# Norm of x: where the transposes' products lie, and when exp of a_log runs

## The chip, the cores and the metric

One core of one Trainium2 chip runs the whole program. The metric is the device time of one execution in microseconds (us); lower is better. Engines: PE is TensorE, whose matmuls show as PE and whose weight loads show as PEld; DVE is VectorE, ACT is ScalarE, POOL is GpSimd, and SP issues most transfers.

## The reference, cut to what matters

The program is one step of a hybrid decoder layer. What is computed around the change:

```python
def _rmsnorm(x, g):
    xf = x.astype(jnp.float32)
    xf = xf * lax.rsqrt(jnp.mean(xf * xf, axis=-1, keepdims=True) + EPS)
    return (xf * g.astype(jnp.float32)).astype(x.dtype)

def _layer(x, ...):
    hn = _rmsnorm(x, norm_g)
    proj = hn @ w_in                     # 1024 -> 13344 columns
    u, v, gate_a, z, xbc, dt_raw, q, gate_x, merge = jnp.split(proj, ...)
    ...
    dt = jax.nn.softplus(dt_raw + dt_bias)
    a = -jnp.exp(a_log)
    y, h_new = _ssd(xh, dt, a, ...)      # decays from cumulative sums of dt * a
    ...
```

The rows of x are 512 of a prompt and 64 of samples; the sizes are D_MODEL 1024, 32 SSD heads, SSD chunks of 128.

## The kernel before, in words

The kernel keeps everything transposed: the model dimension on the 128 partitions, the 576 rows of x along the free axis. Every large product is made from fp32 split into a high and a low part in fp32r (`split`, L96: ACT copies the high part, DVE subtracts), so a block of 128 output columns costs, for each of two halves of 288 rows (`HT`), 24 matmuls: three for each of the 8 pieces of the model dimension (`gemm`, L141, its matmul at L154; `gemm_half`, L159, at L167).

**Order of the work.** A planner lays out each engine's instructions ahead of time, from the program's order and its own guess of durations; the chip then runs each engine's list in that order, with waits between engines. The order on an engine therefore is not the order of the source, and an edit can move instructions that it does not name. A tile of a pool is a buffer that the planner hands out when its first writer is placed, and takes back when its last reader is placed.

**Banks.** In the first part of the kernel, PE's results have 8 banks (`banks(stb, 4, 1, 3)`, L189): 4 for accumulators (`acc_tile`, L71), 1 for `y_tile`, and 3 for small products (`s_tile`, L77). A tile of any kind is one bank of 128 x 512 fp32.

**Norm of x** (L195 to L240). Five tiles of x (four of 128 rows, one of 64) are loaded. Two groups follow one another, tiles 0 to 2 and tiles 3 to 4. For each group: ACT squares and sums (L226); `rsqrt_` (L101) makes the factor, with a Sqrt on ACT (L109); DVE scales the tiles (L230). Then, for each of the 8 pieces k of the model dimension, PE transposes that piece of every tile of the group into one bank (L237), ACT writes the high part `hn_hi` from it, times the norm's weight (L239), and DVE writes the low part `hn_lo` from the same bank (L240). The bank is free again when both have read it. In the first group a piece is 384 columns wide, in the second 192.

**What follows.** The product for dt (L287, 48 matmuls of 32 output columns at L154) needs all of hn: its first half of 288 rows needs the first group alone. ACT adds the bias (L290), PE transposes (L293), and DVE and ACT make softplus of it (L296 to L313): an Exp on ACT at L301, a series on DVE. Then exp of a_log on ACT (L315), dt times that on DVE (L317), and cumulative sums on PE (L319 to L322). The first blocks of xBC are multiplied by `gemm_half` (L167) in between. Sqrt and Exp need different function tables on ACT; a table load is put ahead of the first instruction in ACT's order that needs another table. In the kernel before, that is a_log's Exp (L315).

The helper `run(first, *made)` (L118) orders an instruction behind others; within one engine it only fixes the order there.

Of the kernel before, what the change touches and what calls it, by code (L numbers as in the profile page):

```python
# [11 lines left out]
AF = mybir.ActivationFunctionType  # L12
# [30 lines left out]
def tile_hybrid_step(  # L43
# [8 lines left out]
    V, S, PE, GP, SY = nc.vector, nc.scalar, nc.tensor, nc.gpsimd, nc.sync  # L52
# [18 lines left out]
    def acc_tile():  # L71
        return bank["acc"].tile([P, 512], F32, tag="acc", name="acc")
# [4 lines left out]
    def s_tile():  # L77
        return bank["sps"].tile([P, 512], F32, tag="sps", name="sps")
# [22 lines left out]
    def rsqrt_(pool, r, a, b, tag="nwt", root=False):  # L101

        sh = [r.shape[0], r.shape[1]]
        w = pool.tile([P, P], F32, tag=tag, name="nwt", bufs=2)[:, 0:24].rearrange("p (k c) -> p k c", k=3)
        x, y, t = (w[:sh[0], k, 0:sh[1]] for k in range(3))
        V.tensor_scalar(x, r, a, b, ALU.mult, ALU.add)
        if root:
            V.reciprocal(y, x)
            S.activation(y, y, AF.Sqrt)  # L109
        else:  # L110
            V.tensor_scalar(y.bitcast(I32), x.bitcast(I32), -0.5, 1597463007.0, ALU.mult, ALU.add)
        for _ in range(1 if root else 3):
            V.tensor_tensor(t, y, y, ALU.mult)
            V.scalar_tensor_tensor(t, t, -0.5, x, ALU.mult, ALU.mult)
            V.scalar_tensor_tensor(y, t, 1.5, y, ALU.add, ALU.mult)
        return y

    def run(first, *made):  # L118

        for m in made:  # L120
            tc.add_manual_dep(first.ins, m.ins.name, mybir.DependencyInfo(
                mybir.DependencyClass.NoSync if m.ins.engine == first.ins.engine else mybir.DependencyClass.Sync,
                mybir.DependencyReason.DATA), reason="run")
# [17 lines left out]
    def gemm(w, nk, xh, xl, n=P, width=HT, halves=2):  # L141

        hi, lo = w
        outs = []
        for f in range(halves):
            ps = acc_tile()
            sl = slice(f * width, (f + 1) * width)
            last = 3 * nk - 1
            i = 0
            terms = [[(hi[:, k], xh(k)), (hi[:, k], xl(k)), (lo[:, k], xh(k))] for k in range(nk)]  # L150
            if lo_last[0]:
                terms = [t[0:2] for t in terms] + [t[2:3] for t in terms]
            for a, b in [p for t in terms for p in t]:
                PE.matmul(ps[:n, :width], lhsT=a, rhs=b[:, sl], start=(i == 0), stop=(i == last))  # L154
                i += 1
            outs.append(ps)
        return outs
# [30 lines left out]
    with ExitStack() as stb:  # L188
# [30 lines left out]
        for tiles in ((0, 1, 2), (3, 4)):  # L219
            n = len(tiles)  # L220
            ss = pb.tile([P, 3], F32, tag="ss", name="ss", bufs=2)
            if 4 in tiles:
                GP.memset(ss, 1.0)
            for a, i in enumerate(tiles):
                m = TS if i == 4 else P
                S.activation(junk[:m], xts[i][:m], AF.Square, accum_out=ss[:m, a:a + 1])  # L226
            q = rsqrt_(pb, ss[:, 0:n], 1.0 / D, EPS, "BT", root=True)
            for a, i in enumerate(tiles):
                m = TS if i == 4 else P
                V.tensor_scalar_mul(xts[i][:m], xts[i][:m], q[:m, a:a + 1])  # L230
            c0 = tiles[0] * P
            w = 3 * P if n == 3 else P + TS
            for k in range(KD):
                ps = s_tile()
                for a, i in enumerate(tiles):
                    m = TS if i == 4 else P
                    PE.transpose(ps[:, a * P:a * P + m], xts[i][:m, k * P:(k + 1) * P], ident[:m, :m])  # L237
                g = gcol[:, k:k + 1]
                S.activation(hn_hi[:, k, c0:c0 + w], ps[:, 0:w], AF.Copy, scale=g)  # L239
                V.scalar_tensor_tensor(hn_lo[:, k, c0:c0 + w], ps[:, 0:w], g, hn_hi[:, k, c0:c0 + w], ALU.mult, ALU.subtract)  # L240
# [26 lines left out]
        alog = pb.tile([P, H], F32, name="alog")  # L267
# [19 lines left out]
        ps = gemm(wdt, KD, xh, xl, n=H)  # L287
# [10 lines left out]
        tmp = pb.tile([P, 3, HC], F32, tag="cacc", name="tmp", bufs=2)  # L298
        sa, sb, sc = tmp[:, 0], tmp[:, 1], tmp[:, 2]
        V.scalar_tensor_tensor(sa, dtr, -1.0, dtr, ALU.mult, ALU.max)  # L300
        S.activation(sa, sa, AF.Exp, scale=-1.0)  # L301
        V.tensor_scalar(sb, sa, 2.0, None, ALU.add)
        V.reciprocal(sb, sb)
        V.tensor_tensor(sa, sa, sb, ALU.mult)
# [7 lines left out]
        dtf = dt.rearrange("p c h -> p (c h)")  # L312
        V.scalar_tensor_tensor(dtf, sc, 2.0, dtr, ALU.mult, ALU.add)  # L313
        V.memset(dt[64:128, 4, :], 0.0)
        S.activation(alog, alog, AF.Exp)  # L315
        adt = pb.tile([P, 5, H], F32, tag="t1", name="adt", bufs=2)
        V.scalar_tensor_tensor(adt, dt, -1.0, alog[:, None, :].to_broadcast([P, 5, H]), ALU.mult, ALU.mult)  # L317
        aps = s_tile()
# [1130 lines left out]
    for i in range(4):  # L1449
# [6 lines left out]
        for p_, (c0, cn) in enumerate(pieces):  # L1456
            ps = acc_tile()
# [54 lines left out]
```

## Time and profile before

| what | us |
|---|---|
| median of 3 runs | 1135.39 |
| lowest and highest of them | 1131.92, 1139.5 |
| the profiled execution, its own time | 1134.07 |
| its span, from the first to the last instruction | 1132.3 |
| TensorE busy in the span | 1099.1 |
| mean granted TensorE clock | 0.993 |

The profiled execution's time is 1.8 us more than its span: what lies around the instructions. An engine's timeline gives for each instruction its start, its duration, and in brackets how long the engine had been idle before it and what ended that. Matmuls are pipelined: a matmul's duration is longer than the distance to the next one, so it is the distance between starts that says how fast PE goes. Busy times of PE are modelled from such ends.

### The profile page before, as it was taken

What the parts mean: (1) busy time and instruction counts of PE and PEld (TensorE: products, weight loads), DVE (VectorE), ACT (ScalarE), POOL (GpSimd) and SP (SyncE); (2) the same over time, 40 slices, a digit from 0 to 9 for tenths busy, and PEclk for the clock granted to TensorE, in tenths of its full rate; (3) what the DMA queues carried; (4) which work ended last, traced back from release to release, by engine and by line L of the source; (5) the groups of instructions that cost most, each with busy time, mean ns of one, the idle gap of its engine ahead of it and who ended that gap; (6) DMA issues with size and microseconds to landing.
All of it is one profiled execution on the core that took longest, in us unless ns stands there. A gap on an engine that the chain in (4) does not pass through costs nothing.

```text
span 1132.3 us, 20429 instructions
## 1 busy us (share of the span) xinstructions
PE 1099.1 (97%) x8200; PEld 1022.9 (90%) x8200; DVE 781.2 (69%) x1444; ACT 618.5 (55%) x1291; POOL 25.3 (2%) x109
## 2 busy tenths in 40 slices
PE   5999898999999999999999999999999999999997
PEld 4999797999999999999999778999999999889776
DVE  5679686858678786876536546877965567775743
ACT  6366686777767576775543236335652335564421
POOL 1010000000000000000000000000000000000000
PEclk9999999999999999999999999999999999999999
DMA  5343535254452525445224515441262453456311
GB/s 174 113 101 114 143 113 142 64 174 111 145 149 82 161 62 175 111 144 149 80 88 141 174 67 185 149 149 38 90 218 96 154 161 112 138 171 205 141 47 74
DMA packets 160334, 144.38 MB, mean 128 GB/s; under 512 B 10152, under 2 KB 141264, under 8 KB 160240
## 3 DMA queue, kind: packets, MB, share of 16 engines
q1 hardware_dynamic: 137136, 125.60, 36.6%
q10 hardware_dynamic: 23104, 17.49, 4.9%
q8 instruction: 64, 1.05, 0.4%
q14 instruction: 30, 0.25, 0.1%
HBM read 123.61 MB, written 19.46 MB: 126 GB/s over the span
## 4 chain that ended last, share of the span: by engine, by line
PE 88%; DMA 4%; DVE 3%; ACT 2%; issue 1%; SPq 0%; ACTq 0%; DVEq 0%
PE acc L167 35%; PE acc L926 16%; PE acc L154 12%; PE acc L1056 4%; PE acc L1461 4%; DMA e<-a_scr 3%; PE acc L1121 2%; PE yps L556 2%; PE sps L575 1%; PE sps L652 1%; PE sps L511 1%; PE sps L600 1%; PE sps L540 1%; DVE cacc L426 1%; PE yps L1409 1%
## 5 line engine op out<-in xcount | busy, mean ns | idle before, releaser
L167 PE MATMUL acc<-hn_hi,whi 128*128 128x288 f32 x896 | 272.3, 304 | 0.1
L167 PE MATMUL acc<-hn_hi,wlo 128*128 128x288 f32 x896 | 266.5, 297 | 1.5 <-DVE wlo L99 1.5
L167 PE MATMUL acc<-hn_lo,whi 128*128 128x288 f32 x896 | 266.4, 297 | 0.0
L167 PEld LDWEIGHTS acc<-hn_hi,whi 128*128 128x128 f32 x896 | 170.4, 190 | 1.9 <-issue 1.5
L167 PEld LDWEIGHTS acc<-hn_hi,wlo 128*128 128x128 f32 x896 | 170.1, 190 | 2.0 <-DVE wlo L99 2.0
L167 PEld LDWEIGHTS acc<-hn_lo,whi 128*128 128x128 f32 x896 | 170.5, 190 | 0.4
L98 ACT CAST w<-wraw 128x1024 fp32r<-128x1024 f32 (+1 forms) x64 | 59.2, 942 | 103.2 <-PE acc L926 24.0
L99 DVE TENSOR_TENSOR wlo<-wraw,whi 128x1024 fp32r<-128x1024 f32 x72 | 87.8, 1220 | 29.1 <-ACT whi L98 28.7
L167 PE MATMUL acc<-hb,whi 128*128 128x288 f32 x512 | 104.5, 299 | 0.1
L98 ACT CAST whi<-wraw 128x1024 fp32r<-128x1024 f32 x72 | 75.6, 1050 | 46.1 <-PE acc L167 44.0
L99 DVE TENSOR_TENSOR w<-wraw,w 128x1024 fp32r<-128x1024 f32 x64 | 68.5, 1087 | 35.8 <-ACT w L98 35.3
L926 PE MATMUL acc<-hn_hi,w 128*128 128x288 f32 x512 | 89.4, 301 | 0.0
L926 PE MATMUL acc<-tT,w 128*128 128x288 f32 x576 | 86.2, 298 | 0.0
L426 DVE SCALAR_TENSOR_TENSOR cacc<-raw,cwh,cacc 128x600 f32<-128x600 f32 x96 | 80.4, 838 | 4.7 <-ACT cacc L424 4.0
L167 PEld LDWEIGHTS acc<-hb,whi 128*128 128x128 f32 x512 | 81.6, 188 | 1.0 <-issue 0.6
L926 PEld LDWEIGHTS acc<-tT,w 128*128 128x128 f32 x576 | 78.6, 188 | 0.9 <-issue 0.9
L926 PEld LDWEIGHTS acc<-hn_hi,w 128*128 128x128 f32 x512 | 74.1, 188 | 2.0 <-DVE thx L944 0.4
L167 PE MATMUL acc<-hb,wlo 128*128 128x288 f32 x256 | 75.3, 294 | 0.0
L499 ACT ACTIVATE e<-e,nacs 128x128 f32<-128x128 f32 (+1 forms) x160 | 50.4, 382 | 13.4 <-DVE e L497 13.0
L99 DVE TENSOR_TENSOR w<-S,w 128x1024 fp32r<-128x1024 f32 x32 | 39.1, 1223 | 25.0 <-ACT w L98 25.0
L154 PE MATMUL acc<-ha,w 128*128 128x288 f32 x384 | 51.6, 295 | 0.0
L154 PE MATMUL acc<-hn_hi,w 128*128 128x288 f32 x256 | 51.2, 295 | 0.0
(393 smaller groups left out, 2117.5 us busy)
## 6 DMA issues: line engine op xcount, KB each, us to landing
wraw<-in_w_in_dram SPq DMA_DIRECT2D x44, 1024.0 KB
wraw<-in_w_in_dram SPq DMA_DIRECT2D x16, 512.0 KB
e<-a_scr SPq DMA_DIRECT2D x32, 256.0 KB
h<-in_state_ssm_dram SPq DMA_DIRECT2D x16, 512.0 KB
out_dram<-h ACTq DMA_DIRECT2D x16, 512.0 KB
wraw<-in_w_proj_b_dram SPq DMA_DIRECT2D x8, 1024.0 KB
ebc<-e_scr SPq DMA_DIRECT2D x16, 288.0 KB
wraw<-in_w_mem_kv_dram SPq DMA_DIRECT2D x4, 1024.0 KB
```

Of the source, the lines that this page charges most:

```text
L98: S.copy(hi, v)
L99: (e or V).tensor_tensor(lo, v, hi, ALU.subtract)
L154: PE.matmul(ps[:n, :width], lhsT=a, rhs=b[:, sl], start=(i == 0), stop=(i == last))
L167: PE.matmul(ps[:, 0:HT], lhsT=a[:, k], rhs=b(k)[:, sl], start=(n == 0), stop=(n == 3 * nk - 1))
L426: V.scalar_tensor_tensor(a[:, 0:n], raw[:, i:i + n], cwh[:, i, q:q + 1], a[:, 0:n], ALU.mult, ALU.add)
L499: S.activation(e[:, h, 0:w], e[:, h, 0:w], AF.Exp, bias=nacs[:, c, h0_ + h:h0_ + h + 1])
L511: PE.transpose(tp[:, j * P:(j + 1) * P], xs[:, j, c0:c0 + P], ident)
L556: m = PE.matmul(y4[64 * r:64 * r + 64, i, j], lhsT=xdt[:, h], rhs=e[:, h, 0:w], start=True, stop=True)
L926: PE.matmul(ps[:, 0:HT], lhsT=w[:, r, k], rhs=x(q, k), start=first and n == 0, stop=n == 11, skip_group_check=True)
L1056: PE.matmul(pss[i], lhsT=x(k)[:, c], rhs=w[:, r, k2], start=(k + q == 0), stop=(k == KD - 1 and q == 2))
L1121: PE.matmul(pss[i], lhsT=x[xr], rhs=w[:, r, k2], start=(k + q == 0), stop=(k == KD - 1 and q == 2))
L1461: PE.matmul(ps[:, 0:cn], lhsT=x(k)[:, c], rhs=w, start=(k + q == 0), stop=(k == KD - 1 and q == 2))
```

## The change

Two edits. In the norm of x, the bank for piece k is taken from the three banks for small products when k is odd, and from the four accumulators' banks when k is even, so that up to 7 banks serve the transposes in place of 3. And exp of a_log (L315) is ordered on ACT behind the Exp of softplus (L301).

```diff
             for k in range(KD):
-                ps = s_tile()
+                ps = s_tile() if k % 2 else acc_tile()
                 for a, i in enumerate(tiles):
                     m = TS if i == 4 else P
                     PE.transpose(ps[:, a * P:a * P + m], xts[i][:m, k * P:(k + 1) * P], ident[:m, :m])
...
         V.scalar_tensor_tensor(sa, dtr, -1.0, dtr, ALU.mult, ALU.max)
-        S.activation(sa, sa, AF.Exp, scale=-1.0)
+        made = S.activation(sa, sa, AF.Exp, scale=-1.0)
         V.tensor_scalar(sb, sa, 2.0, None, ALU.add)
...
         V.memset(dt[64:128, 4, :], 0.0)
-        S.activation(alog, alog, AF.Exp)
+        run(S.activation(alog, alog, AF.Exp), made)
         adt = pb.tile([P, 5, H], F32, tag="t1", name="adt", bufs=2)
```

## Rows read from the trace of the kernel before

**Rows 1.** The page: busy time of each engine, and the last chain by engine.
```profile
PE 1099.1 (97%) x8200; PEld 1022.9 (90%) x8200; DVE 781.2 (69%) x1444; ACT 618.5 (55%) x1291; POOL 25.3 (2%) x109
PE 88%; DMA 4%; DVE 3%; ACT 2%; issue 1%; SPq 0%; ACTq 0%; DVEq 0%
```
**Rows 2.** Stretches: start:end, length, each engine's busy us (instructions), TensorE clock, DMA.
```profile
13.20:18.35 5.15, 4.95 (x22) 4.10 (x22) 4.50 (x9) 3.75 (x8) 0.38 (x2) 1.00 0.77 198
18.35:27.20 8.85, 7.95 (x51) 5.12 (x49) 5.82 (x14) 5.83 (x13) 0.00 (x0) 1.00 0.08 19
46.00:49.00 3.00, 3.00 (x15) 3.00 (x14) 1.95 (x6) 2.20 (x5) 0.00 (x0) 0.50 0.49 138
99.00:219.00 120.00, 111.28 (x885) 104.66 (x884) 95.45 (x193) 85.32 (x211) 3.98 (x22) 0.97 0.43 121
```
**Rows 3.** Timeline of PE: start, us, engine, line, output<-inputs, [idle before <-releaser].
```profile
10.69 2.23 PE L237 MATMUL sps<-ident,xbuf 128*128 128x128 f32 x9 [8.07 <-DVE xbuf L230]
13.16 0.45 PE L154 MATMUL acc<-hn_hi,whi 128*32 128x288 f32 x1 [0.24 <-ACT hn_hi L239]
13.81 0.90 PE L237 MATMUL sps<-ident,xbuf 128*128 128x128 f32 x3 [0.20 <-DVE hn_lo L240]
...
14.99 0.84 PE L237 MATMUL sps<-ident,xbuf 128*128 128x128 f32 x3
...
15.87 0.44 PE L154 MATMUL acc<-hn_lo,whi 128*32 128x288 f32 x1
16.11 0.84 PE L237 MATMUL sps<-ident,xbuf 128*128 128x128 f32 x3
...
18.52 0.29 PE L154 MATMUL acc<-hn_lo,whi 128*32 128x288 f32 x1
18.65 0.29 PE L154 MATMUL acc<-hn_hi,wlo 128*32 128x288 f32 x1
...
18.91 0.49 PE L237 MATMUL sps<-ident,xbuf 128*128 128x128 f32 x3
...
20.75 0.32 PE L154 MATMUL acc<-hn_hi,whi 128*32 128x288 f32 x1 [0.30 <-ACT hn_hi L239]
...
22.88 0.32 PE L154 MATMUL acc<-hn_hi,whi 128*32 128x288 f32 x1 [0.42 <-ACT hn_hi L239]
...
40.00 0.46 PE L319 MATMUL sps<-adt,tri 128*128 128x128 f32 x2
...
47.05 0.44 PE L167 MATMUL acc<-hn_hi,wlo 128*128 128x288 f32 x1
47.29 0.44 PE L167 MATMUL acc<-hn_hi,whi 128*128 128x288 f32 x1
```
**Rows 4.** Timeline of ACT: the two table loads, and the instructions beside the second.
```profile
0.80 1.28 ACT L213 ACT_TABLE_LOAD   x1 [0.80 <-PEq L1498]
...
18.71 1.28 ACT L315 ACT_TABLE_LOAD   x1
20.00 0.23 ACT L315 ACTIVATE alog<-alog 128x32 f32<-128x32 f32 x1
20.14 0.56 ACT L239 ACTIVATE hn_hi<-sps,gcol 128x384 fp32r<-128x384 f32 x1
...
30.07 0.49 ACT L290 ACTIVATE dtF<-acc,dtb 32x288 f32<-32x288 f32 x1
32.14 0.34 ACT L301 ACTIVATE tmp<-tmp 128x160 f32<-128x160 f32 x1 [1.58 <-DVE tmp L300]
```
**Rows 5.** Timeline of DVE: the end of the first group, and the last step of dt.
```profile
20.73 0.62 DVE L240 SCALAR_TENSOR_TENSOR hn_lo<-sps,gcol,hn_hi 128x384 fp32r<-128x384 f32 x1 [0.54 <-ACT hn_hi L239]
21.27 0.74 DVE L230 TENSOR_SCALAR xt<-xt,nwt 64x1024 f32<-64x1024 f32 x1
...
39.52 0.33 DVE L317 SCALAR_TENSOR_TENSOR adt<-dt,alog 128x160 f32<-128x160 f32 x1
```
**Rows 6.** Timeline of POOL: the write that the first ACTIVATE at L213 reads.
```profile
0.94 0.20 POOL L84 MEMSET ones<- 128x128 f32 x1
```

## Prediction, made before the run

> **What bounds the kernel now.** First the page: PE is busy for 97% of the span and holds 88% of the chain that ended last, ACT for 55% and DVE for 69% [rows 1]. So an instruction taken from ACT or DVE is worth only what PE waits for it, and a bank only what PE waits for banks. What can be won is idle time of PE, or time in which its clock is low, between its first transposes at 10.69 us and the end of the norm near 27 us.
>
> Second the timeline of PE in that stretch [rows 3]. Nine transposes go out (three pieces k of three tiles: that is all that 3 banks hold), then PE idles 0.24 us, does one matmul of dt, idles 0.20 until DVE has read the first bank, and from 13.81 goes in rounds: three transposes, two matmuls of dt. From 14.99 to 16.11 a round takes 1.12 us. In it PE does not idle: the stretch 13.20 to 18.35 has 4.95 us busy of 5.15 [rows 2]. The matmuls of dt fill what the banks leave open. Later there are two more gaps, 0.30 and 0.42 us, both ended by ACT's `hn_hi` [rows 3]; the whole stretch 18.35 to 27.20 has 8.85 - 7.95 = 0.90 us idle [rows 2]. Idle in all: 0.24 + 0.20 + 0.90 = 1.34 us.
>
> Third the clock. Matmuls of 288 columns start 0.24 us apart at 15.87 and 0.13 us apart at 18.52 [rows 3]. The granted clock is printed as 1.00 for both, but 0.24 is also their distance from 47.05 to 47.29 [rows 3], where 0.50 is granted [rows 2]. I go by the distance: PE is at its lower level, 1.2 GHz, until some 18.35 us, and at 2.4 GHz after it. In the 7.7 us from 10.69 to 18.35 the low level costs about half, 3.6 us: more than all the idle time.
>
> Fourth ACT and DVE. Between two `hn_hi` of the first group ACT loads a table, 1.28 us, and runs a_log's Exp, 0.23 us [rows 4]. The last transposes of that group start at 18.91 and last 0.49, so their bank was full at 19.40, and ACT came to it at 20.14 [rows 3, 4]. DVE's `hn_lo` at 20.73 waits for it, and the scaling of the last tile of x stands behind that, at 21.27 [rows 5].
>
> **The Exp moved.** Out of the norm go 1.28 + 0.23 = 1.51 us of ACT. Last in this place is then the transposes' end at 19.40, so `hn_hi` of the last piece starts 20.14 - 19.40 = 0.74 us earlier, and with it `hn_lo` and the last scaling. PE had dt's matmuls to do until about 20.45, so it gains the gap of 0.30 and a part of the other 0.60 idle. Lower bound 0, upper bound 0.90; I take 0.6.
>
> The load comes back ahead of softplus's Exp at L301. ACT is done at 30.07 + 0.49 = 30.56 and idles 1.58 us until 32.14 [rows 4]. A load needs no data of its instruction: the one at L213 starts at 0.80, before POOL writes at 0.94 what that instruction reads [rows 4, 6]. So 1.28 us fit into 1.58, with 0.30 to spare, and a_log's Exp (0.23) follows L301 and is wanted only at 39.52 [rows 5]. Price 0. If the cover is gone, the load starts when L301 could: 1.28 us late for the whole series on DVE. That series ends at 39.52 + 0.33 = 39.85, and PE takes it up at 40.00 without having idled [rows 3, 5]: only 0.15 us of slack in PE's list, so the loss would be up to 1.28 - 0.15 = 1.1 us.
>
> The Trainium skill speaks against this part: ScalarE: Activation LUTs, What ACT_TABLE_LOAD costs, counts about 1283 ns for the load and about 1380 more for a drain, 2.66 us for each change of table. By that the load would not fit into 1.58 us, but come 1.08 us late and cost some 0.9 us at L319. This trace agrees on the load alone: 1.28 us, and its Exp starts 0.01 us after its end; no drain is seen in it [rows 4].
>
> **The banks.** With 7 banks PE need not stop after nine transposes. A transpose at the low level costs (1.12 - 2 x 0.24) / 3 = 0.213 us. The 15 left of the first group end at 12.92 + 15 x 0.213 = 16.1 us instead of 19.40. The gaps of 0.24 and 0.20 go: 0.44. What is late next is the reading of the banks: ACT takes 0.58 a piece, DVE 0.62, eight pieces from about 12.5 and 13.1 on, with a weight's split and the second group's factor among them, so some 18 to 19 us for the end of the first group. That was 21.35 before (20.73 + 0.62), so the second group can start two to three us earlier. But no work of PE goes away: 24 of dt's matmuls that stood between the transposes now stand behind them, as cover while ACT and DVE read. PE is the bound again, and wins only the 0.44, and the rest of the 0.90 in part: 0.1 more. Bounds: 0 (the planner hands the banks to dt's accumulators, too, and spaces the list as before) and 0.44 + 0.30 = 0.74.
>
> The clock is the open term. From 12.92 on PE would have no gap. Whether that brings the rise forward can't be read from one execution. At best all from 12.92 on is at 2.4 GHz: (18.35 - 12.92) / 2 = 2.7 us won. At worst, where the second group outruns its readers and leaves PE waiting, it comes later; the one low stretch that the trace shows afterwards, about 46 to 49 us [rows 2], bounds this by half of 3 us, 1.5 lost. I take 1.0 won, nearer to the middle of the two ends than to the upper, as dense work is all that the trace shows ahead of 18.35. Likewise that later low stretch may go or come twice when the list before it is laid anew: 1.5 either way; I take 0.
>
> **Sum.** 0.6 + 0.5 + 1.0 = 2.1 us. The profiled execution took 1134.07, its span 1132.3 and 1.8 around it; 1134.07 - 2.1 = 1132.0. That execution lies 1.3 below the median of the runs (1135.39), inside their spread from 1131.9 to 1139.5, and the spread is wider than the sum.
>
> **Rivals.**
> - *The clock rises sooner.* Idle 1.34, clock 2.7, and the low stretch at 46 us gone, 1.5: 5.5 us, 1128.5. For it: the rise at 18.35 came after the rounds without gaps. Against: the time from the last gap (13.81) to it is 4.5 us, so it can hardly be won whole. The Trainium skill (TensorE: Matmul & The Clock Gate, Part 1) says that the low level is the default and that sustained activity releases it, which this trace agrees with (0.24 us, then 0.13 us, after dense work); by it the sum would lean to this case.
> - *Nothing comes of it.* PE's work is the same and dt's matmuls had filled the banks' waits; the clock stays. Within 0.8 us: 1133.3 to 1134.
> - *Slower: the softplus chain.* The place is L319, 0.15 us of slack. It decides once softplus's Exp starts over 0.30 us behind its data, because the planner puts something into the 1.58 us of ACT, or because the first half of dt, now waiting for an accumulators' bank or placed behind the second group's transposes, ends later. Price 1.1 us for the load, and 1.5 with a later clock: 1135 to 1137.
> - *The new order carries on.* From 99 to 219 us, PE idles 120.00 - 111.28 = 8.7 us [rows 2]. There the order decides, and a shift of some us ahead can lay it otherwise: as much as half of it either way, 4.4 us, so 1128 or 1136; with other parts on top over 1% only in rare cases.
>
> **How the numbers follow.** Forecast (1 to 4 us won) 0.50; nothing 0.17; clock sooner 0.12; softplus chain 0.10; order carried on 0.11, either way alike. The likeliest gives 1132. The range takes in the bounds: 1134.07 less 1.34 + 2.7 + 1.5 and a little for the order, 1127, and up to 1134.07 + 1.1 + 1.5 and as much again for the runs' median above the profiled one, 1138. One per cent is 11.4 us, about what a measurement of this kernel can tell from no change. None of the cases reaches it by itself; only the last does, with all else on the same side: faster 0.04, slower 0.03, within 0.93.
>
> **What would show it.** On ACT: no table load between two `hn_hi`, and one between L290 and L301, with L301 at once behind L300. On PE: more than nine transposes ahead of the first matmul of dt, the first group's last transposes near 16 us, matmuls of dt in one run behind them, no gap ended by `hn_hi` near 20.7, L319 some 2 us sooner than 40.00. Where matmuls first stand 0.13 us apart tells the clock's term. It would be wrong if PE idles before the second group's transposes for as long as it had been filled before, if L319 has idle time in front, or if a stretch past 99 us differs by more than the norm does.

## The result, and the profile after

The changed kernel is slower: 1140.45 us median (1136.68 to 1142.91) against 1133.79 for the kernel before, ratio 1.0052 with a 95% interval of 1.0042 to 1.0062. That is 5.9 us, with an interval of 4.8 to 7.0. It is within 1%, as forecast, but on the other side of 1 and outside the range of 1127 to 1138.

The page of the kernel after, its parts 1 and 4, to be read beside [rows 1]:

```profile
PE 1098.7 (96%) x8200; PEld 1021.2 (90%) x8200; DVE 780.0 (68%) x1444; ACT 618.3 (54%) x1291; POOL 26.0 (2%) x109
PE 85%; DMA 6%; DVE 5%; ACT 2%; issue 1%; ACTq 0%; SPq 0%; DVEq 0%
```

The busy times are the same within some 1.2 us. What grew is the share of the last chain that is not PE. Where, the timeline of PE says (columns as in [rows 3]):

```profile
11.59 0.48 PE L237 MATMUL acc<-ident,xbuf 128*128 128x128 f32 x1 [9.02 <-DVE xbuf L230]
...
14.21 0.42 PE L237 MATMUL acc<-ident,xbuf 128*128 128x128 f32 x1
14.42 0.32 PE L237 MATMUL sps<-ident,xbuf 128*128 128x128 f32 x1
14.58 0.27 PE L237 MATMUL acc<-ident,xbuf 128*128 128x128 f32 x1
14.69 0.49 PE L237 MATMUL sps<-ident,xbuf 128*128 128x128 f32 x3
15.01 0.49 PE L237 MATMUL acc<-ident,xbuf 128*128 128x128 f32 x3
16.05 0.55 PE L237 MATMUL sps<-ident,xbuf 128*128 128x128 f32 x3 [0.55 <-DVE hn_lo L240]
21.52 0.47 PE L237 MATMUL acc<-ident,xbuf 128*128 128x128 f32 x1 [4.92 <-DVE xbuf L230]
...
26.36 0.45 PE L154 MATMUL acc<-hn_hi,whi 128*32 128x288 f32 x1
...
27.75 0.44 PE L154 MATMUL acc<-hn_hi,whi 128*32 128x288 f32 x1
27.99 0.44 PE L154 MATMUL acc<-hn_lo,whi 128*32 128x288 f32 x1
...
31.59 0.29 PE L154 MATMUL acc<-hn_lo,whi 128*32 128x288 f32 x1
31.72 0.29 PE L154 MATMUL acc<-hn_hi,wlo 128*32 128x288 f32 x1
...
47.82 0.46 PE L319 MATMUL sps<-adt,tri 128*128 128x128 f32 x2
```

All 24 transposes of the first group go out by 16.6 us, as the banks' edit promised. Then PE has nothing for 4.92 us. The first matmul of dt, which stood at 13.16 before [rows 3], now stands at 26.36, behind all transposes of the second group. And the clock goes up, down and up: transposes start 0.21 us apart until 14.42 and then 0.107 (three in 0.32 us); behind the hole matmuls start 0.24 us apart (27.75 to 27.99), and 0.13 apart only from 31.6 on (31.59 to 31.72). The stretches of the same profile, with columns as in [rows 2], say it with the granted clock:

```profile
13.20:16.60 3.40, 2.85 (x18) 2.38 (x16) 2.08 (x6) 3.07 (x8) 0.02 (x1) 1.00 0.52 136
16.60:21.52 4.92, 0.00 (x1) 0.01 (x1) 4.85 (x11) 2.55 (x6) 0.37 (x2) 0.63 0.80 212
21.52:27.20 5.68, 5.68 (x20) 3.18 (x20) 3.52 (x9) 3.04 (x8) 0.00 (x0) 0.50 0.00 0
27.20:31.40 4.20, 4.20 (x19) 2.97 (x19) 0.60 (x4) 0.00 (x0) 0.00 (x0) 0.50 0.08 23
99.00:219.00 120.00, 110.75 (x895) 104.27 (x894) 96.71 (x192) 85.61 (x211) 3.99 (x22) 0.99 0.43 121
```

In the hole DVE is busy for 4.85 of 4.92 us. Its timeline shows with what (compare [rows 5]):

```profile
18.54 0.61 DVE L240 SCALAR_TENSOR_TENSOR hn_lo<-sps,gcol,hn_hi 128x384 fp32r<-128x384 f32 x1
19.06 0.15 DVE L113 TENSOR_TENSOR nwt<-nwt 128x2 f32<-128x2 f32 x1
19.18 1.23 DVE L99 TENSOR_TENSOR wlo<-wraw,whi 128x1024 fp32r<-128x1024 f32 x1
...
20.70 0.76 DVE L230 TENSOR_SCALAR xbuf<-xbuf,nwt 128x1024 f32<-128x1024 f32 x1
21.37 0.74 DVE L230 TENSOR_SCALAR xt<-xt,nwt 64x1024 f32<-64x1024 f32 x1
```

The scaling of the second group, for which PE waits, stands behind all eight `hn_lo` of the first group and a weight's split of 1.23 us. It starts at 20.70. ACT's list has the same turn: the Sqrt of the second group's factor stands behind all eight `hn_hi` (it stood at 13.93 us before):

```profile
17.96 0.25 ACT L109 ACTIVATE nwt<-nwt 128x2 f32<-128x2 f32 x1
```

In the kernel before, DVE scaled tile 3 while PE still ran dt's matmuls, and PE went on to the second group behind a gap of 0.30 us:

```profile
19.44 0.75 DVE L230 TENSOR_SCALAR xbuf<-xbuf,nwt 128x1024 f32<-128x1024 f32 x1
20.91 0.82 PE L237 MATMUL sps<-ident,xbuf 128*128 128x128 f32 x3
```

**The sum at L319.** In the profile of before, x came a little earlier (first transposes at 10.69 us; in the profiles of all kernels after it between 11.06 and 11.68), so I count from there to L319: 40.00 - 10.69 = 29.31 us before, 47.82 - 11.59 = 36.23 after, 6.92 more. Idle time of PE in the norm: 4.92 + 0.55 = 5.47 us against 1.34, 4.13 more. Time at the low clock: 14.42 - 11.59 and 31.6 - 21.52, in all 12.9 us, against 7.66 - 0.44 = 7.2 of work before; half of the difference is 2.85. 4.13 + 2.85 = 6.98. That it closes so well is in part luck. PE's list also has seven more matmuls of 288 columns ahead of L319 (133 to 126; 0.9 us of work that is only moved). It has fewer turns between transposes and matmuls, which cost time as well: in the kernel before, the first of two matmuls behind transposes starts 0.39 us ahead of the second (15.48 and 15.87 us), against 0.24 without transposes. And `e1_banks_alone` below, with the same loss in time, has L319 only 33.90 us behind its first transposes. Without the moved work 6.0 us are left, about the 5.9 measured. In this execution the hole is the larger part, the clock some 40%.

Behind L319 the two profiled executions take nearly the same time, 1132.3 - 40.00 = 1092.3 us and 1139.3 - 47.82 = 1091.5, so the loss lies ahead of it. That is a balance. The kernel before has three low stretches of 3.4 us there (granted clock 0.50 from about 46, 117 and 199 us), the changed kernel one (from 124 us), which gives it some 3.4 us back, and 0.9 more for the moved work. PE's idle time between 99 and 1125 us takes 2.3 of this again (16.6 us against 14.3); the rest was not followed.

### The profile page after: what moved, and what is told of

Read it like the earlier page. It is cut to its first block, busy times and chain, and to the rows that moved or that the text cites. A ratio compares the mean times of both kernels' runs of the same rounds, so it can differ in the third digit from the quotient of the medians.

```text
span 1139.3 us, 20431 instructions
## 1 busy us (share of the span) xinstructions
PE 1098.7 (96%) x8200; PEld 1021.2 (90%) x8200; DVE 780.0 (68%) x1444; ACT 618.3 (54%) x1291; POOL 26.0 (2%) x109
## 4 chain that ended last, share of the span: by engine, by line
PE 85%; DMA 6%; DVE 5%; ACT 2%; issue 1%; ACTq 0%; SPq 0%; DVEq 0%
PE acc L167 34%; PE acc L926 15%; PE acc L154 12%; DMA e<-a_scr 4%; PE acc L1056 4%; PE acc L1461 4%; PE yps L556 2%; DVE cacc L426 1%; PE acc L1121 1%; PE sps L575 1%; PE sps L540 1%; PE sps L600 1%; PE sps L652 1%; DVE wlo L99 1%; PE sps L511 1%
```

## The experiments

Theory A: the planner hands out the accumulators' banks in the order in which the source asks for them. With the banks' edit the transposes of both groups ask eight times for four banks before dt does, so dt's product loses its place between the groups; the hole that opens there, which DVE's list makes long, costs its length and then the clock. Theory B: the Exp's edit brings a table load ahead of softplus and delays dt and all that follows.

### Each edit alone

`e1_banks_alone` has the banks' edit, and L315 as before:

```diff
-                ps = s_tile()
+                ps = s_tile() if k % 2 else acc_tile()
```

> The banks' edit alone; the Exp of a_log stays where the kernel before has it. Theory A (the bank taken for dt's product): all four accumulators' banks are handed out in turn to the transposes of both groups, dt's product gets one only behind the second group, PE has nothing to do from about 16.6 to 21.5 us and then runs at the low clock. Then this alone costs what the whole change costs: 5 to 8 us more than the kernel before, L319 at about 47 to 48 us in place of 40.0. Theory B (the Exp's table load ahead of softplus delays dt and all behind it): no slower than the kernel before, L319 near 40.

Measured: 1141.23 us, ratio 1.0050 (1.0033 to 1.0067). The same hole of 4.92 us, ended by the same line, and dt's first matmul at 26.28:

```profile
21.44 0.48 PE L237 MATMUL acc<-ident,xbuf 128*128 128x128 f32 x1 [4.92 <-DVE xbuf L230]
```

L319 stands at 45.4, earlier than expected: ten matmuls fewer stand ahead of it than in the changed kernel (123, 1.3 us), and the clock came back at 29.3 here. This edit alone carries the whole loss.

`e2_exp_alone` has the Exp's edit, and three banks (its line at L315; `made` is softplus's Exp, as in the change):

```diff
-        S.activation(alog, alog, AF.Exp)
+        run(S.activation(alog, alog, AF.Exp), made)
```

> The Exp's edit alone; three banks as in the kernel before. Theory A: 0.3 to 1 us faster than the kernel before, since the two gaps of PE that ACT's hn_hi ended (0.30 and 0.42 us) shrink and the table load lies under ACT's idle 1.58 us ahead of L301; L319 between 39 and 40 us. Theory B: slower by 1 us or more, with idle time of PE in front of L319.

Measured: 1136.36 us, ratio 1.0005 (0.9991 to 1.0018): no difference. Theory B falls as the cause. The timelines of ACT and of PE in this kernel:

```profile
20.69 0.32 PE L154 MATMUL acc<-hn_lo,whi 128*32 128x288 f32 x1 [0.15 <-DVE hn_lo L240]
...
21.64 0.52 PE L237 MATMUL sps<-ident,xbuf 128*128 128x128 f32 x3 [0.49 <-DVE xbuf L230]
...
30.18 0.49 ACT L290 ACTIVATE dtF<-acc,dtb 32x288 f32<-32x288 f32 x1
30.68 1.28 ACT L301 ACT_TABLE_LOAD   x1
32.25 0.34 ACT L301 ACTIVATE tmp<-tmp 128x160 f32<-128x160 f32 x1 [0.28 <-DVE tmp L300]
...
41.90 0.46 PE L319 MATMUL sps<-adt,tri 128*128 128x128 f32 x2 [0.27 <-DVE adt L317]
```

The load lies under ACT's wait, as forecast: behind it the Exp still waits 0.28 us for DVE. But the 0.3 to 1 us did not come. The gap of 0.30 us ahead of the second group did not shrink: 0.15 us on `hn_lo` and 0.49 us on the scaling of tile 3 stand in its place, now ended by DVE. L319 was to move forward and stands 1.5 us later, counted from the first transposes (41.90 - 11.06 against 29.31), with 0.27 us idle in front. PE's list has 137 matmuls of 288 columns ahead of L319 there and 126 before: the planner put eleven more in front, 11 x 0.13 = 1.4 us.

### Dt's bank

`e3_first_group` has both edits, but the second group's transposes ask for small products' banks only, so dt is the fifth to ask for an accumulator and not the ninth:

```diff
-                ps = s_tile() if k % 2 else acc_tile()
+                ps = s_tile() if k % 2 or n < 3 else acc_tile()
```

> Both edits, but the second group's transposes take small products' banks only, so dt's first half needs no bank that waits for the second group. Theory A: the hole of 4.9 us is filled with dt's first half again and the clock stays up behind its rise; 7 to 10 us faster than the changed kernel, that is 1 to 4 us faster than the kernel before; L319 at 36.5 to 39. If the loss comes from something else in the seven-bank order (the readers ACT and DVE, a bank that both read), it stays within 2 us of the changed kernel.

Measured: 1138.03 us, ratio 1.0026 (1.0014 to 1.0038). Half of the loss is gone, the expected gain over the kernel before did not come, and L319 stands at 45.8 and not at 36.5 to 39. The order did what theory A says: dt's first half runs from 15.83 to 19.6 us, between the groups. But stretches of this profile, below the start of dt, show what is left:

```profile
15.83 0.37 PE L154 MATMUL acc<-hn_hi,whi 128*32 128x288 f32 x1
...
19.60:21.54 1.94, 0.01 (x1) 0.04 (x1) 1.87 (x5) 0.49 (x1) 0.00 (x0) 1.00 0.72 175
21.54:22.57 1.03, 0.91 (x6) 0.53 (x6) 0.50 (x1) 0.16 (x1) 0.00 (x0) 1.00 0.00 0
22.57:32.81 10.24, 9.93 (x38) 5.95 (x39) 3.62 (x11) 2.99 (x8) 0.00 (x0) 0.50 0.04 11
32.81:40.00 7.19, 7.19 (x54) 6.70 (x53) 4.74 (x10) 3.59 (x6) 0.00 (x0) 1.00 0.46 144
```

dt's 24 matmuls, now at the high clock, are done in under 4 us, and DVE's list has not moved: the second group's transposes start at 21.54, as in the changed kernel. A hole of 1.94 us is left. The clock falls 1.0 us behind its end and is low for 10.2 us. So theory A was incomplete: the bank explains 3 us of the 6, and the rest hangs on a hole much shorter than the one it took away.

### Filling the hole with work that nobody needs

Two kernels put transposes of 128 x 128 in the hole, whose result nobody reads. `e4_fill` adds 44 to the changed kernel, between the groups (`last_t` is the transpose placed last):

```diff
...
+            if n == 3:
+                fill = y_tile()
+                for q_ in range(44):
+                    t_ = PE.transpose(fill[:, 0:P], ident, ident)
+                    if q_ == 0:
+                        run(t_, last_t)
```

> The changed kernel with 44 more transposes of the identity, whose result nobody reads, on PE between the two groups: the hole stays a hole for the kernel's own work, but PE is busy in it. It parts the loss: idle time alone against the clock. If the clock is lost through the hole, matmuls behind 21.5 us start 0.13 us apart and not 0.24, and 3 to 5 us of the loss are gone: L319 at 43 to 45, time 1 to 3 us over the kernel before. If the low clock behind the hole has another cause, L319 stays near 47.8 and the time 5 to 8 us over.

Measured: 1137.16 us, ratio 1.0021 (1.0003 to 1.0040). Two stretches of it, beside those of the changed kernel at nearly the same times:

```profile
16.60:21.57 4.97, 4.97 (x46) 4.76 (x44) 4.90 (x11) 2.60 (x6) 0.39 (x2) 1.00 0.82 211
21.57:27.20 5.63, 5.45 (x40) 4.00 (x40) 3.69 (x12) 2.60 (x8) 0.00 (x0) 1.00 0.07 20
```

The kernel's own work starts as late as in the changed kernel, 21.57 us, but at the full clock: in 5.6 us PE starts 40 matmuls instead of 20, and L319 (L325 in this file) stands at 43.2 instead of 47.8. By the medians 3.5 us of the loss are gone (1.0052 - 1.0021; with both intervals, 1 to 6), about the 2.85 of the sum above. But this profiled execution took 1133.76 us, among the fastest of the twelve, which spread over 9 us in step with the clock: the six with a mean granted clock of 0.997 or more took 1133.5 to 1137.7 us, the three with 0.994 or less 1139.3 to 1142.5. So the filling seems to have kept the clock up in most executions and not in all; where it was low in the longer ones is not on record.

`e6_first_fill` does the same to `e3_first_group` with 20, which read a piece of `hn_hi` and so fall among dt's first half:

```diff
...
+                for q_ in range(20):
+                    t_ = PE.transpose(fill[:, 0:P], hn_hi[:, KD - 1, 0:P].bitcast(F32), ident)
...
```

> The kernel in which only the first group takes accumulators' banks (e3_first_group), with 20 transposes that nobody reads put among dt's first half, so that PE is not idle from 19.6 to 21.5 us. Theory A (that hole of 2 us lets the clock fall, and the fall costs some 5 us): matmuls behind 21.5 us stay 0.13 us apart, 4 to 6 us faster than e3_first_group, that is 1 to 3 us faster than the kernel before. If the clock falls there for another cause: within 1 us of e3_first_group, 0.13 us apart only from about 32 us on.

Measured: 1133.68 us, ratio 0.9984 (0.9970 to 0.9998), 4.8 us better than without the filling, inside the 4 to 6 expected. The 20 transposes keep PE busy for 2.1 us, and the granted clock behind them is 1.00:

```profile
19.25 2.35 PE L244 MATMUL yps<-ident,hn_hi 128*128 128x128 f32 x20
...
13.00:31.40 18.40, 18.01 (x119) 14.87 (x118) 11.41 (x28) 11.08 (x23) 0.39 (x2) 1.00 0.36 95
```

Work without use, put where PE would have idled for 2 us, makes the kernel faster than the one before.

### Where the hole comes from, and a better kernel

`e7_scale_early` is `e3_first_group` with two loops over the groups in place of one: the factors and the scaling of both groups first, then the transposes. Nothing is added.

```diff
                 V.tensor_scalar_mul(xts[i][:m], xts[i][:m], q[:m, a:a + 1])
+        for tiles in ((0, 1, 2), (3, 4)):
+            n = len(tiles)
             c0 = tiles[0] * P
...
```

> As e3_first_group, but the factor and the scaling of the second group stand ahead of the first group's transposes in the source, so that DVE's list has them between hn_lo of the first group and not behind all eight and a weight's split. No work is added. Theory A (the hole comes from DVE's list: the scaling stands behind all hn_lo): the second group's transposes start near 18 us instead of 21.5, no hole, the clock stays up, 1 to 4 us faster than the kernel before. If the readers of the banks are the bound whatever the list: a hole of 1 us or more comes at another place, and the time stays over the kernel before's.

Measured: 1132.94 us, ratio 0.9984 (0.9971 to 0.9996). Timelines of DVE and PE, and two stretches:

```profile
16.53 0.60 DVE L242 SCALAR_TENSOR_TENSOR hn_lo<-sps,gcol,hn_hi 128x384 fp32r<-128x384 f32 x1
17.06 0.74 DVE L230 TENSOR_SCALAR xbuf<-xbuf,nwt 128x1024 f32<-128x1024 f32 x1
17.72 0.74 DVE L230 TENSOR_SCALAR xt<-xt,nwt 64x1024 f32<-64x1024 f32 x1
18.38 0.60 DVE L242 SCALAR_TENSOR_TENSOR hn_lo<-acc,gcol,hn_hi 128x384 fp32r<-128x384 f32 x1
...
18.51 0.27 PE L239 MATMUL sps<-ident,xbuf 128*128 128x128 f32 x1
...
18.00:22.00 4.00, 3.94 (x27) 2.54 (x24) 4.00 (x8) 2.20 (x5) 0.00 (x0) 1.00 0.62 167
22.00:27.00 5.00, 5.00 (x33) 3.34 (x32) 3.18 (x10) 2.54 (x7) 0.00 (x0) 1.00 0.05 17
```

The scaling stands after the fourth `hn_lo` and is done at 18.46 us, some three and a half earlier than in `e3_first_group` (22.04); ACT's Sqrt for it stands behind the first `hn_hi`, at 14.56. The second group's transposes start at 18.51, there is no hole, and from some 17.1 on the norm runs at the full clock. It is faster than the kernel before by 1.8 us (0.5 to 3.3), level with `e6_first_fill` and without its useless work: it beats both kernels. L319 stands at 41.0, 0.2 later than before if counted from the first transposes, but with 140 matmuls ahead of it in place of 126: 14 x 0.13 = 1.8 us of work moved forward, so the norm itself gained 1.6.

`e10_early_seven_both` is the changed kernel with this early scaling alone, so dt is the ninth to ask again (beside `e7_scale_early`):

```diff
-                ps = s_tile() if k % 2 or n < 3 else acc_tile()
+                ps = s_tile() if k % 2 else acc_tile()
```

> The changed kernel, both groups on seven banks, with nothing but the early scaling added. dt's first half still gets its bank only behind the second group. Theory A (what costs is the hole between the groups, and the clock that falls in it): the hole shrinks from 4.9 to some 2 us, as the second group's scaling ends near 18.5; if 2 us are enough to let the clock fall, as in e3_first_group, 2 to 4 us slower than the kernel before; if not, within 1.5 us of it. In either case 2 us or more faster than the changed kernel. If dt's place behind the second group is what costs by itself: no more than 1 us faster than the changed kernel.

Measured: 1136.12 us, ratio 1.0015 (1.0004 to 1.0026): 4.2 us better than the changed kernel, still 1.7 slower than the one before. PE's timeline and stretches:

```profile
17.67 0.33 PE L239 MATMUL acc<-ident,xbuf 128*128 128x128 f32 x1 [0.95 <-DVE xbuf L230]
...
18.00:22.00 4.00, 3.76 (x17) 2.06 (x15) 4.00 (x11) 3.24 (x8) 0.00 (x0) 0.77 0.56 143
22.00:26.00 4.00, 4.00 (x17) 2.46 (x16) 2.42 (x7) 0.42 (x1) 0.00 (x0) 0.50 0.08 25
```

A hole of 0.95 us only, and yet the clock falls, near 20 us, and stays low until about 27. Whether the hole did it or the thin work behind it (17 instructions in 4 us) is not parted here.

Four of the kernels have the Exp's edit and seven banks for the first group, and differ in two things alone. Their ratios to the kernel before:

| | scaling of the second group late | early |
|---|---|---|
| second group on seven banks, dt's bank behind it | 1.0052 (changed kernel) | 1.0015 (`e10_early_seven_both`) |
| second group on three banks, dt's bank free of it | 1.0026 (`e3_first_group`) | 0.9984 (`e7_scale_early`) |

Read down, dt's bank is worth 2.9 and 3.5 us; read across, the place of the scaling is worth 4.2 and 4.8. The two add up: neither alone explains the loss.

`e9_early_three_banks` is the early scaling and the Exp's edit with three banks for all (beside `e7_scale_early`):

```diff
-                ps = s_tile() if k % 2 or n < 3 else acc_tile()
+                ps = s_tile()
```

> e7_scale_early with three banks for all transposes, as the kernel before has them: the Exp's edit and the early scaling, without the banks' edit. If the banks are worth something of their own once DVE's list is right: slower than e7_scale_early by 1 us or more, that is 0 to 1 us faster than the kernel before. If the gain of e7_scale_early is the early scaling's alone: within 0.7 us of it, some 2 us faster than the kernel before.

Measured: 1135.57 us, ratio 1.0005 (0.9995 to 1.0014). Without the banks' edit the early scaling brings nothing: PE waits 0.91 us for the first `hn_hi` with its three banks full, and the clock rises at some 19.2 us instead of 17.1 (three transposes in a row take 0.84 us at 17.87 and 0.60 at 18.99).

```profile
14.68 0.45 PE L154 MATMUL acc<-hn_hi,whi 128*32 128x288 f32 x1 [0.91 <-ACT hn_hi L241]
```

So the banks are worth something, some 2 us between 1.0005 and 0.9984, but only with both the other list on DVE and dt's bank left free.

### A start that was to be warm

`e5_warm` puts 48 transposes of the identity on PE of the kernel before, while x is loading:

```diff
+        warm = y_tile()
+        for _ in range(48):
+            PE.transpose(warm[:, 0:P], ident, ident)
```

> The kernel before, with 48 transposes of the identity, which nobody reads, on PE from about 2.6 us on, while x is still loading. It prices the low clock ahead of 18.35 us by itself. Theory A (the clock is the larger term): the norm's matmuls stand 0.13 us apart from the start, up to half of the 7.7 us at the low level is won, less what ACT and DVE then bound: 1.5 to 3.5 us faster than the kernel before. If ACT and DVE bound the norm and the clock is worth nothing there: within 0.5 us of it, PE idling between its transposes instead.

Measured: 1136.28 us, ratio 1.0005 (0.9993 to 1.0017). It decides nothing: with the added instructions the planner put the split of a weight ahead of the first `hn_hi` on ACT. That split waited for its transfer and started at 16.31 us; PE idled 3.36 us, until 17.89, and the clock was low again from 13 us on. `e8_warm_early`, with the same start on `e7_scale_early`, met the same kind of thing (a weight's split ahead of the first `hn_hi` on ACT, and its 1.23 us on DVE ahead of the first `hn_lo`):

> e7_scale_early with the 48 transposes of e5_warm at the start: both parts together, the candidate for a kernel that beats both. Theory A: the two gains add in part, 3 to 6 us faster than the kernel before. If ACT and DVE become the bound of the norm (16 hn_hi and 16 hn_lo, some 8 us of DVE), no better than the better one of the two.

Measured: 1134.33 us, ratio 0.9992 (0.9978 to 1.0005), no better than `e7_scale_early`. One row of its PE, and the stretch behind it:

```profile
18.18 0.32 PE L154 MATMUL acc<-hn_hi,whi 128*32 128x288 f32 x1 [1.80 <-DVE hn_lo L245]
...
18.18:23.00 4.82, 4.82 (x33) 3.44 (x33) 4.37 (x9) 2.79 (x7) 0.00 (x0) 1.00 0.50 131
```

In this execution (1130.44 us, the fastest of the twelve) a hole of 1.80 us, hardly shorter than that of `e3_first_group`, did not let the clock fall. It even rose within the hole: 0.84 is granted from 16.38 to 18.18 us, 0.50 from 13.54 to 16.96.

What the low clock ahead of 18.35 us is worth by itself stays open: no run had the full clock there with the rest of the order unchanged.

## Why the prediction was wrong

- **The step that failed** is in the part on the banks: 24 of dt's matmuls "now stand behind them, as cover while ACT and DVE read". They stand behind the second group's transposes, not the first's, and cover nothing: PE idles 4.92 us there. The part did ask what is late next, and answered DVE's and ACT's reading, with the end of the first group at 18 to 19 us (measured: 19.15), "so the second group can start two to three us earlier". It started 9.93 us behind the first transposes (21.52 - 11.59) against 10.22 before (20.91 - 10.69). The part had put a weight's split and the second group's factor among the reading; both came behind it, and the scaling behind them. Nor did it count who asks for an accumulators' bank: eight transposed pieces, then dt. The source has both orders, though the planner's lists need not follow it. The wrong place of dt cost 2.9 to 3.5 us (`e3_first_group`, `e7_scale_early` against `e10_early_seven_both`), the late scaling 4.2 to 4.8 (`e10_early_seven_both`, `e7_scale_early`).
- **The gap of 0.44 us** that was to go did go, but a wait of 0.55 us on `hn_lo` came, since the eighth piece still needs one of the seven banks back, and 4.92 behind it. Forecast 0.5 won, measured 4.1 lost in idle time.
- **The clock** was the open term, between 2.7 won and 1.5 lost. The rise did come sooner, 2.8 us behind the first transpose instead of 7.7. How much of that is the edit's can't be told from one profile: in `e1_banks_alone`, `e3_first_group` and `e4_fill`, whose PE does the same up to there, it came 4 to 5 us behind. What was mis-sized is the bound of the loss: it went by one low stretch of 3 us, at 46 us (the trace of before has two more, at 117 and 199 us), but behind the hole the clock stayed low for 10.1 us. So the early rise was worth less than the fall.
- **The rival that came** was named, inside the softplus chain ("placed behind the second group's transposes"), and priced at 1.1 us for the table load and 1.5 for a later clock. The price of that misplacement was PE's own idle time and the low clock behind it, 6.9 us at L319.
- **The Exp's part** was right about the cover (the load under the 1.58 us, 0.28 to spare; `e2_exp_alone`). The Trainium skill's count of 2.66 us for a change of table (ScalarE: Activation LUTs, What ACT_TABLE_LOAD costs) is borne out in that run for the load alone: it takes 1.28 us, starts 0.01 us behind the instruction before it, and the Exp behind it waits for DVE and for nothing else. The gain of 0.6 us was wrong: `e2_exp_alone` is no faster. DVE's scaling of tile 3 ended the gap ahead of the second group there, 0.49 us in place of 0.30.
- **The signs to look for** held in part: no load between two `hn_hi`, more than nine transposes ahead of dt, the first group's last near 16 us. L319 did not come 2 us sooner but 7.8 later, and the sign against was there, PE idle ahead of the second group's transposes.

## What to carry to other kernels

When an edit gives a stage more buffers of a shared kind, list who asks for that kind behind it in the source, and what work had been filling the waits that the old, smaller number made: that filling may be the next in the queue. Then follow the list of every engine that feeds the next stage one instruction past the point where the edit's stage ends. And price a gap of TensorE not by its length alone: here a gap of 2 us was followed by 10 us at half the clock, and filling it with useless work won 4.8 us.

## What the runs showed of the hardware

- A short idle time of PE let the clock fall, and it stayed at 1.2 GHz for long although PE was busy again: 4.92 us idle, then 10.1 us low (the changed kernel; 7.9 in `e1_banks_alone`); 1.94 us idle, then 10.2 us low, from 1.0 us behind the hole on (`e3_first_group`). With the hole filled there is no fall in the profiles (`e4_fill`, `e6_first_fill`: granted clock 1.00). The Trainium skill (TensorE: Matmul & The Clock Gate, Part 1) has the low level as the default that returns after idle time; these traces agree on that, and the long stay behind a hole is what I had not expected. Not every hole did it: 1.80 us in `e8_warm_early` did not.
- The mean granted clock of all executions, not only of the profiled ones, goes the same way: 0.989 to 0.994 in the changed kernel, 0.991 to 0.993 in `e1_banks_alone`, 0.992 to 0.995 in `e3_first_group` and `e10_early_seven_both`, but 0.996 to 0.999 in `e6_first_fill` and 0.995 to 0.998 in `e7_scale_early`; the kernel before has 0.994 to 0.999 beside the experiments.
- From the first transposes on, the clock took between 2.8 us (the changed kernel) and 7.7 (the kernel before, `e9_early_three_banks`) to rise.
- What PE did in the low stretch of the changed kernel was thin: 20 matmuls and 20 weight loads in the 5.68 us from 21.52. Whether the thin work kept the clock low was not tried. In `e4_fill` the second group's transposes behind the filled hole did not make it fall.
- The first part of each trace prints a granted clock of 1.00 although matmuls stand 0.24 us apart, as they do where 0.50 is printed; the distance between starts is the safer sign there.
